# The fourth cross-attention head's probabilities turned by VectorE and put in place over DRAM, with its scores' maximum taken sooner

## The chip, the core and the metric

The kernel runs on one core of a Trainium2 chip. The metric is device time in microseconds (us) of one execution; lower is better. Five engines work side by side, each through its own list of instructions in order: TensorE (PE, with its weight loads as PEld), VectorE (DVE), ScalarE (ACT), GpSimd (POOL) and SyncE (SP, which here only issues DMAs). They wait for each other through semaphores.

## What is computed

The kernel is one decoder layer for 256 tokens of width 1024: a token mixer with causal attention, a cross-attention into 256 memory tokens, and a gated feed-forward network, each followed by a layer norm. All of it is float32. The change lies in the cross-attention alone, which has four heads of width 256:

```python
q = (h @ w_xq).reshape(B_, S_, XATTN_HEADS, XATTN_HEAD_DIM)
s = jnp.einsum('bshd,bmhd->bhsm', q, k, ...) * (XATTN_HEAD_DIM ** -0.5)
p = jax.nn.softmax(s, axis=-1)
o = jnp.einsum('bhsm,bmhd->bshd', p.astype(v.dtype), v).reshape(B_, S_, D)
return o @ w_xo
```

The scores and the probabilities `p` come out with the tokens on the partitions, and the product with `v` needs them with the memory tokens on the partitions. So each head's 256 x 256 probabilities have to be turned.

## The kernel before, in words

**Products.** A float32 product is made of three matmuls. Every operand is split into a high part (a cast on ACT, line 495 for activations and 148 for weights) and a low part (a subtraction on DVE, lines 496 and 150); `three` (lines 388 to 393) then issues high by high (L391), high by low (L392) and low by high (L393).

**The weight stream.** `Stream` keeps one list of weight tiles w0, w1, ... in order of use. SP loads raw tiles (L124, names like `w66r`) as the low half of an older tile has been made; ACT and DVE split them (`w59h`, `w59l`). Each step of a projection asks for its tile and, while the stream isn't held, splits one more, so the splits of the tiles to come stand in ACT's and DVE's lists between the work of the cross-attention. A high tile takes the room of one that TensorE has finished with.

**Order of the work.** Nothing reorders the instructions: the Python program is the order of every engine's list. `run(gen, n)` takes n steps of a projection's generator, and the calls between such steps are placed by hand.

**One head of the cross-attention** goes through these steps (h is its number, 0 to 3):

- `xscores(h)` (L1005 to 1017): twelve matmuls (L1012) into one PSUM bank `xs`; then `negmax` on DVE (L646, tile `mx`), `exps` on ACT (L635, two activations with their sums), and `scaled` on DVE (a reciprocal at L640 and two multiplications at L642), which leaves the probabilities in the tile `xpr`.
- `xprobs_out(h)` (heads 0 to 2): DVE turns the blocks of 32 x 32 into a tile `xs` (L527), and POOL issues the DMA of it to DRAM (`xd`, L530).
- `xprobs_in(h)` (heads 0 to 2): POOL waits for `xd` to have landed and issues four DMAs that bring the blocks back to SBUF in their places (`xr`, L538).
- `xprobs_split(h)` (heads 0 to 2): ACT casts `xr` into the high half of `xst` (L495), DVE makes the low half (L496).
- `xprobs_pe(h)` (head 3 alone) does in place of the three steps above: four transposes on TensorE into a PSUM bank `xpt` (L1035), which ACT and DVE split into `xst`.
- `xattend(h)`: twelve matmuls into a bank `xo` (L391 to 393), which ACT and DVE split into `oTh` and `oTl`.

The tiles `xs`, `xr` and `xst` share three buffers of one tag (`pair`); a new one takes a buffer whose last reader stands earlier in the program.

**The output projection** `xo` (L1071) takes the weight rows w51 to w54, for the outputs of heads 0 and 1, in its first eight steps, and w55 to w58 after the last head is there. The program around the change (L1070 to 1083) runs `xattend(0)`, `xprobs_split(1)`, `xscores(3)`, `xprobs_in(2)`, two steps, `xattend(1)`, four steps, `xprobs_split(2)`, `xprobs_pe(3)`, two steps, `xattend(2)`, `xattend(3)`, and then the rest of the projection with the second layer norm.

Of the kernel before, what the change touches and what calls it, by code (L numbers as in the profile page):

```python
# [8 lines left out]
F32 = mybir.dt.float32  # L9
F32R = mybir.dt.float32r  # L10
# [4 lines left out]
P = 128  # L15
D = 1024
S = 256
T = S // P
# [15 lines left out]
PR_BUFS = 7  # L34
# [6 lines left out]
def r32(t):  # L41
    return t.bitcast(F32)


class Stream:
# [122 lines left out]
    def next(self):  # L168

        i = len(self.tiles)  # L170
        return i + (2 if i < len(self.items) and self.items[i][0] == "sums" else 1)
# [40 lines left out]
def decoder_layer(  # L212
# [3 lines left out]
    nc = tc.nc  # L216
# [3 lines left out]
    sp = ctx.enter_context(tc.tile_pool(name="small", bufs=3))  # L220
# [10 lines left out]
    def bank(name):  # L231
        return pb.tile([P, 512], F32, tag="b", name=name)
# [137 lines left out]
    ident = cp.tile([P, P], F32, name="ident")  # L370
# [17 lines left out]
    def three(ps, w, y, start, stop, part=False):  # L388

        (wa, wb), (ya, yb) = w, y  # L390
        nc.tensor.matmul(ps, wa, ya, start=start, stop=False, skip_group_check=part)  # L391
        nc.tensor.matmul(ps, wa, yb, start=False, stop=False, skip_group_check=part)  # L392
        nc.tensor.matmul(ps, wb, ya, start=False, stop=stop, skip_group_check=part)  # L393

    def pair(hl, *ix):
        return hl[0][ix], hl[1][ix]
# [89 lines left out]
    def run(gen, n=None):  # L486

        while n is None or n > 0:
            if next(gen, gen) is gen:
                return False  # L490
            n = None if n is None else n - 1
        return True

    def split(h, l, ps):
        nc.scalar.copy(h, ps)  # L495
        nc.vector.tensor_sub(l, ps, r32(h))  # L496
# [25 lines left out]
    def turned(blocks, n, name, queue=nc.sync):  # L522

        st = sp.tile([P, 4, n, 32], F32, name=f"{name}s", tag="pair", bufs=3)
        for at, src in blocks:
            m = src.shape[1]
            nc.vector.transpose(st[:, :, at:at + m, :].rearrange("p j m b -> p m j b"),  # L527
                                src.rearrange("p m (j b) -> p m j b", b=32))
        via = hp.tile([P, 4, n * 32], F32, name=f"{name}d")
        queue.dma_start(via, st.rearrange("p j m b -> p j (m b)"))  # L530
        return via

    def landed(via, n, name, queue=nc.sync, raw=None):

        if raw is None:
            raw = sp.tile([P, 4, n, 32], F32, name=f"{name}r", tag="pair", bufs=3)
        for j in range(4):
            queue.dma_start(raw[32 * j:32 * (j + 1)].rearrange("p i m b -> p i (m b)"),  # L538
                              via[:, j, :].rearrange("(i a) r -> a i r", i=4))
        return raw  # L540
# [91 lines left out]
    def exps(dst, src, mx, sign=1.0):  # L632
        sm = sp.tile([P, 2], F32, name="sm", bufs=6)
        for j in range(2):
            nc.scalar.activation(dst[:, j, :], src[:, j, :], AF.Exp, bias=mx[:, j:j + 1], scale=sign,  # L635
                                 accum_out=sm[:, j:j + 1])
        return sm

    def scaled(dst, sm):
        nc.vector.reciprocal(sm, sm)  # L640
        for j in range(2):
            nc.vector.tensor_scalar(dst[:, j, :], dst[:, j, :], sm[:, j:j + 1], None, op0=OP.mult)  # L642

    def negmax(src):
        mx = sp.tile([P, 2], F32, name="mx", bufs=6)
        nc.vector.tensor_reduce(mx, src, op=OP.max, axis=AX.X, negate=True)  # L646
        return mx
# [254 lines left out]
    def project(chunks, get, held, pieces=PIECES):  # L902

        acc = {piece: accbank("acc") for piece in PIECES}
        if pieces != PIECES:
            (*_, (_, _, c), _), last = pieces, PIECES[-1]
            acc[pieces[-2]], acc[pieces[-1]] = acc[last][:, :c - last[1]], bank("acc")[:, :last[2] - c]
        head, rest = chunks[:-held], chunks[-held:]  # L910
        done = sum(ws.rows(numbers) for numbers in head)
        if head:
            yield from proj_rows(acc, head, get, PIECES, True, pieces != PIECES, True)
        ws.prepare(ws.used + AHEAD)
        ws.held = True
        for piece in pieces:
            yield from proj_rows(acc, rest, lambda k: get(done + k), [piece], not head or piece[1] % 512 != 0, True,
                                 piece == pieces[-1], bool(head) and pieces != PIECES)
            yield piece, acc[last] if pieces != PIECES and piece == pieces[-2] else acc[piece]
# [77 lines left out]
    xqT, xpr, xpt, turnsx = {}, {}, {}, {}  # L997
# [7 lines left out]
    def xscores(h):  # L1005
        ps = bank("xs").rearrange("p (t s) -> p t s", t=2)
        for low in range(2):
            for t in range(T):
                for kk in range(2):
                    w = xqT[h][low][:, kk, t * P:(t + 1) * P]  # L1010
                    for n in range(2 - low):
                        nc.tensor.matmul(ps[:, t, :], w, xkT[n][:, 2 * h + kk], start=not (low or t or kk or n),  # L1012
                                         stop=bool(low and kk), skip_group_check=True)
        pr = sp.tile([P, 2, T, P], F32, name="xpr", tag="pr", bufs=PR_BUFS)
        by_t = pr.rearrange("p s t b -> p t s b")
        scaled(by_t, exps(by_t, ps.rearrange("p t (s b) -> p t s b", s=2), negmax(ps)))
        xpr[h] = pr

    def xprobs_out(h):
        turnsx[h] = turned([(0, xpr[h].rearrange("p s t b -> p (s t) b"))], 4, "x", nc.gpsimd)  # L1020

    def xprobs_in(h):
        turnsx[h] = landed(turnsx[h], 4, "x", queue=nc.gpsimd)

    def xprobs_split(h):
        raw = turnsx[h].rearrange("p i m b -> p m i b")
        st = sp.tile([P, 2, 2, S], F32R, name="xst", tag="pair", bufs=3)
        xpt[h] = st[:, 0], st[:, 1]
        split(*[x.rearrange("p s (t i b) -> p (s t) i b", t=T, i=4) for x in xpt[h]], raw)

    def xprobs_pe(h):
        pp = bank("xpt").rearrange("p (s t) -> p s t", s=2)
        for s in range(2):
            for t in range(T):
                nc.tensor.transpose(pp[:, s, t * P:(t + 1) * P], xpr[h][:, s, t, :], ident)  # L1035
        st = sp.tile([P, 2, 2, S], F32R, name="xst", tag="pair", bufs=3)
        xpt[h] = st[:, 0], st[:, 1]
        split(*xpt[h], pp)

    def xattend(h):  # L1040
        po = bank("xo").rearrange("p (d t) -> p d t", d=2)
        for dd in range(2):
            for s in range(2):
                c = h * 256 + dd * P
                three(po[:, dd, :], pair(xv, ALL, s, slice(c, c + P)), pair(xpt[h], ALL, s), s == 0, s == 1)
        split(oT[0][:, 2 * h:2 * h + 2, :], oT[1][:, 2 * h:2 * h + 2, :], po)
# [2 lines left out]
    run(xq[0])  # L1049
    xv_split(1)  # L1050
    run(xq[1], 5)
    xscores(0)
    xprobs_out(0)
    run(xq[1])
    run(xq[2], 3)
    xprobs_in(0)
    run(xq[2], 2)
    xscores(1)
    xprobs_out(1)
    run(xq[2])  # L1060
    run(xq[3], 3)
# [1 line left out]
    run(xq[3], 1)  # L1063
    xprobs_split(0)
    run(xq[3], 1)
    xscores(2)
    xprobs_out(2)
    run(xq[3])

    h2 = ap.tile([P, T, D], F32, tag="a8", name="h2")  # L1070
    xo = project(c_xo, lambda k: (oT[0][:, k], oT[1][:, k]), 4)  # L1071
    xattend(0)
    xprobs_split(1)
    xscores(3)
    xprobs_in(2)
    run(xo, 2)
    xattend(1)
    run(xo, 4)
    xprobs_split(2)
    xprobs_pe(3)  # L1080
    run(xo, 2)
    xattend(2)
    xattend(3)

# [376 lines left out]
```

## Time and profile before

| what | value |
|---|---|
| median of 3 runs | 363.35 us (363.15 to 363.68) |
| the profiled execution | 364.67 us, of which its span is 362.9 us |
| TensorE busy in the span | 357.4 us (98%) |
| VectorE busy | 313.8 us (86%) |
| ScalarE busy | 204.2 us (56%) |
| GpSimd busy | 76.9 us (21%) |
| granted clock of TensorE, mean | 0.998 |

The span is the part of the execution that the profile covers; the 1.8 us around it are not seen. Times in the rows below are us from the start of the span. The part that the change touches lies between 150 and 172 us. A matmul's busy time runs until its modelled end, and the next one has begun before that, so TensorE's pace is read from the starts of its matmuls.

### The profile page before, as it was taken

What the parts mean: (1) busy time and instruction counts of PE and PEld (TensorE: products, weight loads), DVE (VectorE), ACT (ScalarE), POOL (GpSimd) and SP (SyncE); (2) the same over time, 40 slices, a digit from 0 to 9 for tenths busy, and PEclk for the clock granted to TensorE, in tenths of its full rate; (3) what the DMA queues carried; (4) which work ended last, traced back from release to release, by engine and by line L of the source; (5) the groups of instructions that cost most, each with busy time, mean ns of one, the idle gap of its engine ahead of it and who ended that gap; (6) DMA issues with size and microseconds to landing.
All of it is one profiled execution on the core that took longest, in us unless ns stands there. A gap on an engine that the chain in (4) does not pass through costs nothing. (4 is left out here: it accounts for less than half of the span.)

```text
span 362.9 us, 5453 instructions
## 1 busy us (share of the span) xinstructions
PE 357.4 (98%) x1836; PEld 304.2 (84%) x1836; DVE 313.8 (86%) x481; ACT 204.2 (56%) x324; POOL 76.9 (21%) x92
## 2 busy tenths in 40 slices
PE   9999999999999999999999999999999999999994
PEld 8888888887888899988888878888888888888883
DVE  5878999984999898765879959999999999879995
ACT  5767776374462565464128617538646654675921
POOL 1000009400010003320010024054044123303283
PEclk9999999999999999999999999999999999999999
DMA  7997379697965996935105896798798789777113
GB/s 243 417 418 287 116 268 330 171 349 187 417 256 185 362 381 226 338 124 178 58 0 204 318 307 217 230 343 278 235 331 266 262 303 298 275 237 246 57 60 116
DMA packets 35771, 89.75 MB, mean 247 GB/s; under 512 B 4256, under 2 KB 14112, under 8 KB 35616
## 3 DMA queue, kind: packets, MB, share of 16 engines
q1 hardware_dynamic: 34688, 87.57, 68.5%
q0 software_dynamic: 624, 1.57, 1.3%
q8 instruction: 14, 0.23, 0.2%
q10 hardware_dynamic: 432, 0.26, 0.2%
q14 instruction: 13, 0.11, 0.1%
HBM read 82.05 MB, written 7.34 MB: 246 GB/s over the span
## 5 line engine op out<-in xcount | busy, mean ns | idle before, releaser
L1128 POOL TENSOR_TENSOR sraw<-gr 128x128 f32<-128x128 f32 x10 | 10.6, 1058 | 104.3 <-DMA gr<-gd 71.2
L878 POOL TENSOR_TENSOR rs<-mv,mhalf 128x1 f32<-128x1 f32 x6 | 3.8, 637 | 66.2 <-DVE mv L876 66.2
L731 POOL TENSOR_TENSOR win<-upad 128x271 f32<-128x271 f32 x4 | 3.5, 880 | 52.7 <-DVE upad L765 52.7
L1129 POOL TENSOR_TENSOR sraw<-sraw,gr 128x128 f32<-128x128 f32 x10 | 12.1, 1205 | 0.8
L496 DVE TENSOR_TENSOR gTl<-gr,gTh 128x512 fp32r<-128x512 f32 x11 | 8.6, 779 | 2.7 <-ACT gTh L495 2.7
L495 ACT CAST h2Th<-tp 128x512 fp32r<-128x512 f32 x4 | 2.2, 587 | 14.5 <-PE tp L515 7.6
L495 ACT CAST S<-sraw 128x384 fp32r<-128x384 f32 (+1 forms) x10 | 5.3, 534 | 8.8 <-POOL sraw L1130 8.8
L495 ACT CAST gTh<-gr 128x512 fp32r<-128x512 f32 x11 | 6.8, 617 | 5.0 <-DMA gr<-gd 5.0
L530 POOL DMA_DIRECT2D xd<-xs x3 | 1.9, 628 | 33.2 <-DVE xs L527 33.2
L1108 ACT ACTIVATE sg<-pg 128x256 f32<-128x256 f32 x22 | 7.6, 378 | 1.7 <-PE pg L393 1.7
L1109 DVE TENSOR_TENSOR sg<-sg,pg 128x256 f32<-128x256 f32 x22 | 8.4, 414 | 0.1
L538 POOL DMA_DIRECT2D xr<-xd x12 | 6.6, 556 | 8.9 <-DMA xd<-xs 6.5
L635 ACT ACTIVATE xpr<-xs,mx 128x256 f32<-128x256 f32 x8 | 3.7, 469 | 8.3 <-DVE mx L646 8.3
L635 ACT ACTIVATE pr<-pr,mx 128x256 f32<-128x256 f32 (+1 forms) x12 | 5.5, 460 | 4.4 <-DVE mx L681 4.4
L527 DVE STREAM_TRANSPOSE gs<-sg 128x512 f32<-128x512 f32 x11 | 7.7, 702 | 0.1
L1133 POOL TENSOR_TENSOR S<-gr,sraw 128x128 f32<-128x128 f32 x8 | 7.6, 950 | 0.0
L1130 POOL TENSOR_TENSOR sraw<-gr 128x128 f32<-128x128 f32 x10 | 7.6, 760 | 0.0
L883 DVE SCALAR_TENSOR_TENSOR r<-r,mv,g 128x512 f32<-128x512 f32 (+1 forms) x10 | 7.0, 730 | 0.2
L164 POOL TENSOR_TENSOR w138l<-t,w138h 128x1024 fp32r<-128x1024 f32 x1 | 4.2, 4209 | 13.1 <-ACT w138h L163 13.1
L496 DVE TENSOR_TENSOR S<-sraw,S 128x384 fp32r<-128x384 f32 (+1 forms) x10 | 5.8, 576 | 1.3 <-ACT S L495 1.3
L776 ACT COPY pr<-pxk 128x256 f32<-128x256 f32 x8 | 2.6, 378 | 7.2 <-PE pxk L431 7.2
L869 DVE BATCH_NORM_STATS2 st<-r 128x6 f32<-128x512 f32 (+1 forms) x10 | 6.4, 637 | 0.3
(1399 smaller groups left out, 1421.8 us busy)
## 6 DMA issues: line engine op xcount, KB each, us to landing
gd<-gs SPq DMA_DIRECT2D x11, 256.0 KB, 5.8
gr<-gd SPq DMA_DIRECT2D x44, 64.0 KB, 2.0
pd<-ps SPq DMA_DIRECT2D x4, 384.0 KB, 4.3
pt<-pd SPq DMA_DIRECT2D x16, 96.0 KB, 7.2
g<-in_ln_g SPq DMA_DIRECT2D x3, 512.0 KB, 6.0
b<-in_ln_b SPq DMA_DIRECT2D x3, 512.0 KB, 7.7
wr<-in_w_qkv SPq DMA_DIRECT2D x5, 256.0 KB, 4.5
mr<-in_mem_t SPq DMA_DIRECT2D x1, 1024.0 KB, 11.5
```

What stands on the lines that cost most here:

```text
L495: nc.scalar.copy(h, ps)
L496: nc.vector.tensor_sub(l, ps, r32(h))
L527: nc.vector.transpose(st[:, :, at:at + m, :].rearrange("p j m b -> p m j b"), src.rearrange("p m (j b) -> p m j b", b=32))
L538: queue.dma_start(raw[32 * j:32 * (j + 1)].rearrange("p i m b -> p i (m b)"), via[:, j, :].rearrange("(i a) r -> a i r", i=4))
L635: nc.scalar.activation(dst[:, j, :], src[:, j, :], AF.Exp, bias=mx[:, j:j + 1], scale=sign, accum_out=sm[:, j:j + 1])
L883: nc.vector.scalar_tensor_tensor(r, r, self.mv[:, 0:1], gb["g", self.i][:, s], op0=OP.subtract, op1=OP.mult)
L1108: nc.scalar.activation(sg, ps[:, :CW].rearrange("p (f b) -> p f b", f=2), AF.Silu, bias=0.0, scale=1.0)
L1109: nc.vector.tensor_mul(sg, sg, ps[:, CW:].rearrange("p (f b) -> p f b", f=2))
L1128: nc.gpsimd.tensor_add(s1, a21, a22)
L1129: nc.gpsimd.tensor_sub(s2, s1, a11)
L1130: nc.gpsimd.tensor_sub(s3, a11, a21)
L1133: nc.gpsimd.tensor_sub(s4_raw, a12, s2)
```

## The change

Head 3 gets the same steps as the other three: `xprobs_out(3)`, `xprobs_in(3)` and `xprobs_split(3)` stand for `xprobs_pe(3)`, which is gone. `xscores` is cut in two: the call issues the matmuls and the maximum, and what it returns issues the exponentials and the scaling. For heads 0 to 2 both are called at once. For head 3 the split of head 1's probabilities stands between them, so that on DVE the maximum comes before that split. The four steps after `xattend(1)` are taken as two and two, with `xprobs_in(3)` between, and the split of head 3's probabilities comes after the last two steps, not before them.

```diff
--- before.py
+++ after.py
@@ -1011,10 +1011,15 @@
                     for n in range(2 - low):
                         nc.tensor.matmul(ps[:, t, :], w, xkT[n][:, 2 * h + kk], start=not (low or t or kk or n),
                                          stop=bool(low and kk), skip_group_check=True)
-        pr = sp.tile([P, 2, T, P], F32, name="xpr", tag="pr", bufs=PR_BUFS)
-        by_t = pr.rearrange("p s t b -> p t s b")
-        scaled(by_t, exps(by_t, ps.rearrange("p t (s b) -> p t s b", s=2), negmax(ps)))
-        xpr[h] = pr
+        mx = negmax(ps)
+
+        def softmax_rest():
+            pr = sp.tile([P, 2, T, P], F32, name="xpr", tag="pr", bufs=PR_BUFS)
+            by_t = pr.rearrange("p s t b -> p t s b")
+            scaled(by_t, exps(by_t, ps.rearrange("p t (s b) -> p t s b", s=2), mx))
+            xpr[h] = pr
+
+        return softmax_rest
 
     def xprobs_out(h):
         turnsx[h] = turned([(0, xpr[h].rearrange("p s t b -> p (s t) b"))], 4, "x", nc.gpsimd)
@@ -1027,15 +1032,6 @@
         st = sp.tile([P, 2, 2, S], F32R, name="xst", tag="pair", bufs=3)
         xpt[h] = st[:, 0], st[:, 1]
         split(*[x.rearrange("p s (t i b) -> p (s t) i b", t=T, i=4) for x in xpt[h]], raw)
-
-    def xprobs_pe(h):
-        pp = bank("xpt").rearrange("p (s t) -> p s t", s=2)
-        for s in range(2):
-            for t in range(T):
-                nc.tensor.transpose(pp[:, s, t * P:(t + 1) * P], xpr[h][:, s, t, :], ident)
-        st = sp.tile([P, 2, 2, S], F32R, name="xst", tag="pair", bufs=3)
-        xpt[h] = st[:, 0], st[:, 1]
-        split(*xpt[h], pp)
 
     def xattend(h):
         po = bank("xo").rearrange("p (d t) -> p d t", d=2)
@@ -1049,13 +1045,13 @@
     run(xq[0])
     xv_split(1)
     run(xq[1], 5)
-    xscores(0)
+    xscores(0)()
     xprobs_out(0)
     run(xq[1])
     run(xq[2], 3)
     xprobs_in(0)
     run(xq[2], 2)
-    xscores(1)
+    xscores(1)()
     xprobs_out(1)
     run(xq[2])
     run(xq[3], 3)
@@ -1063,22 +1059,26 @@
     run(xq[3], 1)
     xprobs_split(0)
     run(xq[3], 1)
-    xscores(2)
+    xscores(2)()
     xprobs_out(2)
     run(xq[3])
 
     h2 = ap.tile([P, T, D], F32, tag="a8", name="h2")
     xo = project(c_xo, lambda k: (oT[0][:, k], oT[1][:, k]), 4)
     xattend(0)
+    rest = xscores(3)
     xprobs_split(1)
-    xscores(3)
+    rest()
     xprobs_in(2)
+    xprobs_out(3)
     run(xo, 2)
     xattend(1)
-    run(xo, 4)
+    run(xo, 2)
+    xprobs_in(3)
+    run(xo, 2)
     xprobs_split(2)
-    xprobs_pe(3)
     run(xo, 2)
+    xprobs_split(3)
     xattend(2)
     xattend(3)
 
```

## Rows read from the trace of the kernel before

**Rows 1.** TensorE's waits in the whole span: us in total, times, longest.

```profile
PE busy L550 <- PEq L1425: 0.8, 1, 0.8
PE left L1402 <- ACT mean L1375: 0.5, 1, 0.5
```

**Rows 2.** Timeline of PE: start, us, engine, line, operation, tiles, count.

```profile
163.76 0.39 PE L393 MATMUL acc<-w53h,oTl 128*128 128x512 f32 x1
163.98 0.60 PE L1035 MATMUL xpt<-ident,xpr 128*128 128x128 f32 x4
164.34 0.48 PE L391 MATMUL acc<-w54h,oTh 128*128 128x512 f32 x1
164.65 0.40 PE L392 MATMUL acc<-w54l,oTh 128*128 128x512 f32 x1
164.89 0.40 PE L393 MATMUL acc<-w54h,oTl 128*128 128x512 f32 x1
```

**Rows 3.** Timeline, 150 to 160 us; brackets: idle before, and what ended it.

```profile
150.57 0.71 DVE L527 STREAM_TRANSPOSE xs<-xpr 128x512 f32<-128x512 f32 x1
...
151.58 0.56 POOL L530 DMA_DIRECT2D xd<-xs  x1 [2.29 <-DVE xs L527]
...
153.73 0.64 PE L1012 MATMUL xs<-xkTh,xq 128*128 128x256 f32 x4
...
155.63 0.62 ACT L495 CAST xst<-xr 128x512 fp32r<-128x512 f32 x1 [2.07 <-DMA xr<-xd]
...
156.23 2.17 POOL L538 DMA_DIRECT2D xr<-xd  x4 [4.09 <-DMA xd<-xs]
...
156.28 0.69 DVE L496 TENSOR_TENSOR xst<-xr,xst 128x512 fp32r<-128x512 f32 x1 [2.00 <-ACT xst L495]
...
156.89 0.69 DVE L646 TENSOR_REDUCE mx<-xs 128x2 f32<-128x512 f32 x1
...
157.62 0.47 ACT L635 ACTIVATE xpr<-xs,mx 128x256 f32<-128x256 f32 x1 [1.36 <-DVE mx L646]
...
158.87 0.62 DVE L642 TENSOR_SCALAR xpr<-xpr,sm 128x256 f32<-128x256 f32 x2
```

**Rows 4.** Landings of xd (all three); then xr of heads 0, 1, 2, issues (ns).

```profile
DMA to landing us min/median/max: 2.4/2.6/4.1
...
L538 POOL DMA_DIRECT2D xr<-xd x4: 548/558/608, 141.3 to 143.0; - x4
...
DMA to landing us min/median/max: 2.4/3.0/3.3
...
L538 POOL DMA_DIRECT2D xr<-xd x4: 548/548/553, 147.1 to 148.7; - x4
...
DMA to landing us min/median/max: 6.3/6.5/6.7
...
DMA to landing us min/median/max: 2.1/2.1/2.2
```

**Rows 5.** Busy us by stretch: PE, PEld, DVE, ACT, POOL; PEclk, DMA share, GB/s.

```profile
140.00:145.00 5.00, 5.00 (x44) 5.00 (x44) 3.84 (x8) 2.62 (x7) 2.81 (x5) 1.00 0.82 270
145.00:150.00 5.00, 5.00 (x44) 5.00 (x43) 3.42 (x7) 2.82 (x7) 2.17 (x4) 1.00 0.91 333
...
164.00:166.00 2.00, 2.00 (x12) 1.74 (x11) 1.01 (x2) 1.38 (x2) 0.00 (x0) 1.00 0.85 295
```

**Rows 6.** Timeline, 160 to 169 us; SPq is SP's DMA queue.

```profile
160.86 0.33 SPq L124 DMA_DIRECT2D w66r<-in_w_gu  x1
...
161.40 1.06 ACT L148 CAST w61h<-w61r 128x1024 fp32r<-128x1024 f32 x1 [0.40 <-PE acc L393]
...
165.10 1.05 ACT L148 CAST w62h<-w62r 128x1024 fp32r<-128x1024 f32 x1
...
166.19 1.23 DVE L150 TENSOR_TENSOR w62l<-w62r,w62h 128x1024 fp32r<-128x1024 f32 x1 [0.26 <-ACT w62h L148]
...
168.75 0.28 PE L392 MATMUL xo<-xst,xv 128*128 128x256 f32 x1
```

## The prediction

> **What bounds the kernel now.** I first read the list of TensorE's waits. It has three lines over the whole span, and the two longest are 0.8 and 0.5 us [rows 1]: TensorE is almost never without work, and none of the three lines belongs to the cross-attention or the feed-forward network. So TensorE's instruction list sets the time. A matmul taken off that list shortens the kernel by its own pitch; work added to another engine costs nothing until TensorE waits for it. The next views were TensorE's timeline around the transposes [rows 2], for the prize, and the timelines of ACT, DVE, POOL and SP from 150 to 169 us with the landings of head 0 to 2's DMAs, to see whether the longer way for head 3 still ends before TensorE asks for it.
>
> **What is removed: four transposes on TensorE.** From the last matmul of w53 to the second of w54 there are 0.89 us (163.76 to 164.65); without the transposes these would be two pitches of 0.24 us (164.65 to 164.89) [rows 2]. So 0.89 - 0.48 = 0.41 us come off TensorE's list. The bounds are 0.36 us (start of the transposes to start of the next matmul) and their busy time of 0.60 us. Nothing hides this: before and after, TensorE goes from one matmul to the next, so all that follows moves forward by 0.41 us if no new wait appears. The split of head 3's probabilities into high and low parts stays, one cast and one subtraction of the same shape, only with a source in SBUF in place of PSUM; I cost that at nothing.
>
> **What is moved: the maximum.** Head 3's scores end at 153.73 + 0.64 = 154.37. DVE then stood idle for 2.00 us until head 1's low half at 156.28, and the maximum came behind that, at 156.89 [rows 3]. Put ahead, it runs from 154.4 to 155.1, inside the idle time, and delays nothing behind it. ACT's next item is still the cast at 155.63, which waits for head 1's blocks from DRAM; the exponentials start behind it, at 155.63 + 0.62 = 156.25, where they started at 157.62: 1.37 us sooner. Were that gain lost, every time below would move later by up to 1.37.
>
> **What is added: DVE's turn, one DMA out, four in.** The scaling ended at 158.87 + 0.62 = 159.49 [rows 3]; 1.37 sooner is 158.12. The turn takes 0.71 us on DVE (158.83). Behind it on DVE stand the split of w59 and head 1's low output, which profit by 1.37 us and give back 0.71. POOL issues the DMA 0.30 us after the turn (head 2: turn over at 151.28, issue at 151.58): 159.13. POOL is free by then; head 2's four issues end at 156.23 + 2.17 = 158.40. That DMA lands 2.6 us later (heads 0 to 2: 2.4 to 4.1) [rows 4]: 161.73, and POOL starts the four loads 0.55 us behind a landing (head 2: 151.58 + 4.1 = 155.68, start 156.23), at 162.28. The last of the four is issued 1.65 us after the first (141.3 to 143.0 and 147.1 to 148.7), at 163.93.
>
> How long that last load takes is the one large unknown. Head 2's took 2.1 to 2.2 us, head 0's 2.4 to 3.3, head 1's 6.3 to 6.7 [rows 4]. The DMA engines' share beside them was 0.82 for head 0 and 0.91 for head 1, and it is 0.85 between 164 and 166 us [rows 5]. That is nearest to head 0, so I take its median of 3.0 and keep 2.1 and 6.7 as ends. It gives 166.9. ACT starts a cast about 0.2 us behind a landing (head 1: 148.7 + 6.7 = 155.4, cast at 155.63): 167.1. SP's queue is not touched, but its loads are paced by DVE: w66, issued at 160.86 once DVE was done with w59 [rows 6], goes out up to 0.9 us sooner and meets the DMA to DRAM; that is in the range of 2.4 to 4.1.
>
> **What stands ahead on ACT and DVE, and what TensorE waits for.** The new split comes behind the split of w62. ACT stood idle for 0.40 us until TensorE released a tile for w61's cast at 161.40 [rows 6]; w62's waits likewise for w53, whose last matmul ends at 163.76 + 0.39 = 164.15. So it starts near 164.2 in place of 165.10, takes 1.05 us and leaves ACT free at 165.3; DVE has done its half (1.23 us, [rows 6]) by 166.5. Neither holds back a cast at 167.1. From cast to low half ready there are 0.65 + 0.69 = 1.34 us (155.63 to 156.28, then the subtraction) [rows 3]: 168.44. TensorE's second matmul of head 3's product with v reads that low half; it stood at 168.75 [rows 6], now 168.75 - 0.41 = 168.34. So TensorE waits 0.10 us, and the sum is -0.41 + 0.10 = -0.31 us. Behind the late cast on ACT and DVE stand head 2's outputs, needed only behind head 3's product, so they add no wait of their own.
>
> The profiled execution took 364.67 us, 362.9 of it span, 1.3 above the median of 363.35; the sum concerns the span and I take it off the median: 363.35 - 0.31 = 363.04.
>
> **A rule against it.** While head 0's four loads were issued, DVE was busy for 3.84 of 5 us [rows 5], and an issue took 548 to 608 ns, against 548 to 553 for head 1 [rows 4]: 60 ns at most of hindrance. The Trainium skill, SBUF — State Buffer, section on the two separate sides, warns that GpSimd can be locked out by some VectorE instructions, so that a DMA issued from its queue waits for its descriptors, and names about 620 ns alone against about 3100 beside a copy. By that figure, as an estimate, one such DMA would cost 2.5 us more and the kernel would come out slower. The trace of heads 0 to 2 does not bear it out.
>
> **The rivals.**
> - *All hidden.* The last load lands as head 2's did, 2.1 to 2.8 us after its issue; the cast starts by 166.9 and nothing waits: -0.41, up to -0.6 with the larger bound: 362.75 to 362.95. For it: the weight loads are spread wider once w66 and w67 go out sooner. I count it with the forecast, since the two differ by less than the runs do; likewise a wait of up to 0.41.
> - *The way over DRAM is late.* Weight loads hold up the four loads, or the DMA out. The point from which it decides is a landing 3.3 us after the last issue: then TensorE's wait of 0.4 eats the prize, and each further tenth is lost in full. With head 2's 4.1 out and head 0's 3.3 in, the cast comes at 168.9 and the wait is 1.9: 363.35 - 0.41 + 1.9 = 364.8. With head 1's 6.7 in, the cast comes at 170.8 and the wait is 3.8: 366.7. For it: a DMA share of 0.85 there. Against it: head 0, with 0.82, stayed at 3.3, and only the 0.91 beside head 1 went with 6.7 [rows 4, 5].
> - *POOL's issues are held by DVE.* Each of the five issues could wait for a DVE instruction of up to 1.23 us, that of w62's size; three of them waiting in full put the cast at 170.8, a wait of 3.8: 366.7. Against it: the 60 ns above. It is the mechanism that the page of the Trainium skill named above describes.
> - *The maximum isn't really sooner.* Something on DVE or ACT keeps the exponentials at 157.62; the cast then comes 1.37 later, at 168.5, a wait of 1.5: 364.4. Against it: 2.00 us of idle DVE at the right place.
> - *More than the transposes.* Earlier splits on ACT and DVE take further small waits off TensorE. Its list of waits has nothing in the stages from here to the last layer norm, so I see at most 0.1 us more; a gain beyond 0.73 would have no source that I can name.
>
> **How the numbers follow.** Forecast with its hidden end and with waits up to 0.41: 0.72, its own range 362.8 to 363.35. DRAM way late: 0.16, of which 0.06 ends within 0.73 us of before. Held issues: 0.02. Maximum not sooner: 0.04. More than that: 0.06. A measurement of this kernel can tell about 0.2%, 0.73 us, from no change. Faster by over that: 0.06. Slower: 0.10 + 0.02 + 0.04 - 0.02 (a maximum only partly sooner stays within) = 0.14. The same: 0.80. The range goes from 362.7 (the larger bound of the prize) to 364.2, into the late cases until about 0.15 is left out.
>
> **What would show it.** After: no transposes at L1035; w54's matmuls directly behind w53's at 0.23 to 0.24 us; the maximum near 154.5 and the exponentials near 156.25; a DMA to DRAM near 159.1; four loads from 162.3 to 164.4; the cast of head 3 between 166.4 and 167.5; the gap of TensorE ahead of head 3's product at most some tenths. A gap of over 0.4 us there, or loads that land more than 3.3 us after issue, makes the forecast of a small gain wrong; a gain of over 0.7 us would show a wait of TensorE that I haven't seen.

## The result: slower by 0.66%, where a gain of 0.1% was forecast

| | median | runs | spread |
|---|---|---|---|
| before | 363.46 us | 7 | 363.15 to 364.47 |
| after | 365.55 us | 7 | 364.73 to 367.28 |

The ratio of after to before is 1.0066, with a 95% interval of 1.0051 to 1.0081. The forecast was 363.04 us in a range from 362.7 to 364.2, with a chance of 0.14 for slower by over 0.2%. The median lies 1.35 us above the upper end of the range. The spread is a result too: the seven runs of the kernel before lie within 1.3 us, those of the changed one within 2.6.

The profiled execution of after took 364.95 us with a span of 362.8, against 364.67 and 362.9 before. Two things stand behind these numbers. The time outside the span, which no trace shows, grew: it is 1.7 to 1.9 us in all 79 executions of before whose span is on record, and 2.1 to 2.2 us in all 18 of after, 0.37 us more in the mean. So of the 2.1 us between the medians some 0.4 lie outside the span. And against that execution of after, that of before had lost 0.5 us ahead of the cross-attention and 0.3 behind it, so the two traces can't be compared by their ends. The cross-attention alone can be compared, from the first matmul of head 0's scores to the first of w59 (the feed-forward network): 181.87 - 131.45 = 50.42 us before, 182.11 - 130.92 = 51.19 us after.

**The profile after.** The page's busy times, and its line of the DMA queue that POOL issues to (packets, MB, share of the 16 engines):

```profile
PE 356.4 (98%) x1832; PEld 304.1 (84%) x1832; DVE 315.1 (87%) x482; ACT 205.2 (57%) x324; POOL 78.9 (22%) x97
q0 software_dynamic: 832, 2.10, 1.8%
```

TensorE's list of waits over the whole span of after (in total, times, longest), which answers to [rows 1]:

```profile
PE busy L550 <- PEq L1425: 0.8, 1, 0.8
PE xo L391 <- ACT xst L495: 0.6, 1, 0.6
PE left L1402 <- ACT mean L1375: 0.5, 1, 0.5
PE xo L392 <- DVE xst L496: 0.3, 1, 0.3
```

Two lines are new, and both say `xo` and `xst`: TensorE waits for the high half (ACT) and then for the low half (DVE) of a head's turned probabilities. The timeline of PE shows where. First the place where the transposes were [rows 2], then the seam between head 2's and head 3's product (start, us, engine, line, operation):

```profile
163.02 0.39 PE L393 MATMUL acc<-w53h,oTl 128*128 128x512 f32 x1
163.24 0.39 PE L391 MATMUL acc<-w54h,oTh 128*128 128x512 f32 x1
163.47 0.39 PE L392 MATMUL acc<-w54l,oTh 128*128 128x512 f32 x1
...
167.28 0.28 PE L393 MATMUL xo<-xst,xv 128*128 128x256 f32 x1
168.18 0.38 PE L391 MATMUL xo<-xst,xv 128*128 128x256 f32 x1 [0.62 <-ACT xst L495]
168.90 0.38 PE L392 MATMUL xo<-xst,xv 128*128 128x256 f32 x1 [0.34 <-DVE xst L496]
```

The prize is there: w54 follows w53 at 0.22 to 0.23 us. But these products start every 0.12 us, and the two marked starts come 0.90 and 0.72 behind the one ahead. TensorE waits 0.78 + 0.61 = 1.39 us. (The brackets say less, since they count from the modelled end of the last matmul.)

The chain that ends there, from the timelines of DVE, ACT and POOL, answers to [rows 3]:

```profile
153.80 0.69 DVE L646 TENSOR_REDUCE mx<-xs 128x2 f32<-128x512 f32 x1
...
155.09 0.47 ACT L635 ACTIVATE xpr<-xs,mx 128x256 f32<-128x256 f32 x1
...
156.99 0.71 DVE L527 STREAM_TRANSPOSE xs<-xpr 128x512 f32<-128x512 f32 x1
...
158.00 0.56 POOL L530 DMA_DIRECT2D xd<-xs  x1 [0.34 <-DVE xs L527]
161.10 1.09 POOL L538 DMA_DIRECT2D xr<-xd  x2 [2.54 <-PE acc L393]
162.35 1.09 POOL L538 DMA_DIRECT2D xr<-xd  x2
...
163.44 1.05 ACT L148 CAST w62h<-w62r 128x1024 fp32r<-128x1024 f32 x1 [1.15 <-PE acc L393]
167.50 0.62 ACT L495 CAST xst<-xr 128x512 fp32r<-128x512 f32 x1 [3.01 <-DMA xr<-xd]
```

The landings of head 3's DMA out, and the issues (ns) and landings of its four loads, which answer to [rows 4]:

```profile
DMA to landing us min/median/max: 2.4/2.4/2.4
...
L538 POOL DMA_DIRECT2D xr<-xd x4: 548/550/553, 161.1 to 162.9; - x4
...
DMA to landing us min/median/max: 4.2/4.4/4.5
```

The reader is to see that everything up to the four loads was in time, and that ACT, done with w62 at 164.5, then stood idle for 3.01 us until the last of them landed. They took 4.2 to 4.5 us, the last 4.5; the sum had 3.0.

### The profile page after: what moved, and what is told of

The parts are those of the page before. It is cut to its first block, busy times and chain, and to the rows that moved or that the text cites. A ratio compares the mean times of both kernels' runs of the same rounds, so it can differ in the third digit from the quotient of the medians.

```text
span 362.8 us, 5464 instructions
## 1 busy us (share of the span) xinstructions
PE 356.4 (98%) x1832; PEld 304.1 (84%) x1832; DVE 315.1 (87%) x482; ACT 205.2 (57%) x324; POOL 78.9 (22%) x97
## 5 line engine op out<-in xcount | busy, mean ns | idle before, releaser
L1128 POOL TENSOR_TENSOR sraw<-gr 128x128 f32<-128x128 f32 x10 | 8.8, 875 | 103.3 <-DMA gr<-gd 76.4
L538 POOL DMA_DIRECT2D xr<-xd x16 | 8.8, 557 | 11.6 <-ACT xst L495 4.2
L1130 POOL TENSOR_TENSOR sraw<-gr 128x128 f32<-128x128 f32 x10 | 11.0, 1097 | 0.0
L1129 POOL TENSOR_TENSOR sraw<-sraw,gr 128x128 f32<-128x128 f32 x10 | 10.7, 1066 | 0.8
L1012 PE MATMUL xs<-xkTh,xq 128*128 128x256 f32 x32 | 6.4, 283 | 0.0
```

Of the source, the lines that this page charges most:

```text
L1128: nc.gpsimd.tensor_add(s1, a21, a22)
L1129: nc.gpsimd.tensor_sub(s2, s1, a11)
L1130: nc.gpsimd.tensor_sub(s3, a11, a21)
```

## The experiments

Theory A: TensorE waits for head 3's halves, since its four loads land late, and they land late because of the weight loads beside them. Rival B: the way over DRAM is too long in itself, whatever else is on the DMA engines. Rival C: the time is lost elsewhere, and the wait is only a part of it. All edits are to the changed kernel, where nothing else is said.

**The changed kernel again, eight traces in all.** Nothing is edited.

> The changed kernel once more, to see how its loss is spread. Theory A (TensorE waits for head 3's low and high halves, because the four loads from DRAM land late): the wait of TensorE ahead of head 3's product, 1.4 us in the first trace, is found again and is larger in a longer execution; 364.7 to 367.3 us. Rival C (the time is lost elsewhere, the wait is only a part of it): the wait stays near 1.4 us in a longer execution and other gaps of TensorE make up the rest.

It took 366.5 us in the median of 5 runs (363.99 to 367.99), ratio 1.0068 (1.0040 to 1.0097). But its traced execution was the shortest of the five, with the same wait as the first. So more single executions were traced, for a long one.

> The changed kernel, one more look, for an execution longer than the two traced so far (waits of 1.38 us, spans 361.8 and 362.8). Theory A: in an execution of 365 us and more of span, the loads of head 3 land 5 us or more after their issue, the wait of TensorE is 3 us or more, and its granted clock falls behind that wait as in the run with the late maximum. Rival C: the wait is again 1.4 us and the longer time lies elsewhere.

> As the look before it: another execution of the changed kernel, same expectations.

These two were short ones as well (364.14 and 364.77). Four more followed:

> The changed kernel; if this execution is over 366 us, theory A expects loads that land 6 us or so after their issue, a wait of TensorE of 3 us or more and a granted clock of about a half for some 2 us behind it; rival C expects the wait of 0.9 to 1.4 us again and the rest elsewhere.

> The changed kernel once more; for an execution over 366 us the same expectations as for the look before this one.

> The changed kernel once more; for an execution over 366 us the same expectations as for the two looks before this one.

> The changed kernel once more; for an execution over 366 us the same expectations as for the three looks before this one.

The eight executions, in order of the wait. "Wait" is what the first two starts of head 3's product come late, as worked out above; "stage" runs from head 0's scores to w59; "clock" is the lowest granted clock in any 2 us from 160 to 178 us.

| time | loads' landing, min to max | wait | stage | clock |
|---|---|---|---|---|
| 364.14 | 3.2 to 4.0 | 0.89 | 50.71 | 1.00 |
| 364.77 | 3.2 to 4.2 | 1.09 | 50.91 | 1.00 |
| 364.95 | 4.2 to 4.5 | 1.39 | 51.19 | 1.00 |
| 363.99 | 3.9 to 4.5 | 1.39 | 51.21 | 1.00 |
| 365.59 | 3.7 to 5.0 | 1.93 | 51.73 | 1.00 |
| 367.45 | 4.2 to 4.8 | 2.12 | 53.69 | 0.50 |
| 368.25 | 4.3 to 5.4 | 2.75 | 54.24 | 0.50 |
| 368.73 | 2.8 to 3.3 | 3.06 | 54.36 | 0.50 |

Up to a wait of 1.93 the stage is 49.72 us (the same stage without any wait, from the runs below) plus the wait plus 0.1. In the last three it is 1.5 to 1.7 us more than that. (The four longest of the eight were all taken on one chip, so the chip may have a part in the spread; but the five runs from 363.99 to 367.99 come from one chip as well.) The execution of 368.25 us shows where the rest comes from. Its timeline of PE, and its busy times by stretch (PE, PEld, DVE, ACT, POOL; then granted clock, DMA share, GB/s):

```profile
167.46 0.28 PE L393 MATMUL xo<-xst,xv 128*128 128x256 f32 x1
169.72 0.38 PE L391 MATMUL xo<-xst,xv 128*128 128x256 f32 x1 [1.99 <-ACT xst L495]
170.45 0.38 PE L392 MATMUL xo<-xst,xv 128*128 128x256 f32 x1 [0.34 <-DVE xst L496]
...
172.24 0.63 PE L391 MATMUL acc<-w55h,oTh 128*128 128x512 f32 x1
172.67 0.63 PE L392 MATMUL acc<-w55l,oTh 128*128 128x512 f32 x1
```

```profile
168.00:170.00 2.00, 0.28 (x1) 0.19 (x1) 0.29 (x1) 0.94 (x2) 0.00 (x0) 1.00 0.63 238
170.00:172.00 2.00, 1.66 (x11) 1.55 (x11) 1.00 (x2) 0.16 (x1) 0.00 (x0) 0.84 0.04 12
172.00:174.00 2.00, 2.00 (x8) 1.61 (x7) 0.69 (x1) 1.52 (x2) 0.00 (x0) 0.50 0.00 0
```

TensorE was busy for 0.28 us of the two from 168 to 170. Behind that the granted clock fell to 0.50, its lower level of 1.2 GHz, and w55's matmuls came every 0.43 us, not every 0.23, until the clock was back between 174 and 176. So in these executions a late landing is paid twice, once as the wait and once as slow matmuls behind it. That is the case in the longest executions alone: of the 12 in the two groups of runs, the mean granted clock was 0.994 or 0.995 in the four from 367.12 us up, and 0.997 to 0.999 in the other eight, those at the two medians among them. Rival C falls for the larger part of the spread, since the long executions are those with the long wait (363.99 and 364.95, with the same wait, differ by 1 us elsewhere). It holds for the 0.37 us outside the span, which every execution of after has. The last one of the table was late for another reason. Its loads landed in 3.3 us at most, but they could not be issued before 165.00. Head 2's DMA out had taken 5.4 us (4.1 before), and POOL, which issues in order, came to head 3's DMA out at 159.60. That one took 4.7 us; the load of w66 was issued 0.15 us behind it, where 0.6 to 0.8 us lay between them in the other seven traces, with 2.4 to 2.5 us to its landing:

```profile
159.60 0.56 POOL L530 DMA_DIRECT2D xd<-xs  x1
165.00 1.09 POOL L538 DMA_DIRECT2D xr<-xd  x2 [4.84 <-issue]
```

**The weight loads wait for head 3's loads.**

```diff
     xattend(1)
-    run(xo, 2)
     xprobs_in(3)
-    run(xo, 2)
+    seen = hp.tile([P, 2], F32, name="seen")
+    nc.sync.dma_start(seen, turnsx[3][:, 0, 0, 0:2])
+    run(xo, 4)
```

> POOL's loads stay, but SP waits for them to have landed before it loads w67, w68 and w69 (a small DMA that reads from all four parts stands ahead on SP's queue); only w66 can run beside them. Theory A with traffic as the cause: landings 2.1 to 2.6 us after the issue as for head 2, no wait of TensorE ahead of head 3's product, 363.0. Rival B: landings still over 4 us, 365 to 366. If the postponed weight loads themselves come late, TensorE waits for w67 or w68 after 182 us instead.

It took 363.36 us, ratio 0.9998 (0.9986 to 1.0011). Landings of the four loads, ACT's cast behind them, and SP's queue:

```profile
DMA to landing us min/median/max: 2.1/2.2/2.3
```

```profile
166.12 0.62 ACT L495 CAST xst<-xr 128x512 fp32r<-128x512 f32 x1 [1.13 <-DMA xr<-xd]
...
166.18 0.33 SPq L1078 DMA_DIRECT2D seen<-xr  x1
166.60 0.38 SPq L124 DMA_DIRECT2D w67r<-in_w_gu  x1
```

The same four loads, issued by the same engine as late as 162.0 to 163.8, land in 2.1 to 2.3 us once w67 and w68 aren't beside them, and head 3's wait is gone. Theory A with traffic as the cause stands, and rival B falls. The weight loads, held back by up to 6 us, are missed by nobody: TensorE has no new wait behind them. The stage took 50.21 us in this trace, 0.49 over the one without a wait, as it held 0.3 us of another wait, for head 1's low half, and 0.1 of a slower start behind it.

**Only w68 and w69 wait.** The small DMA stands behind w67 on SP's queue.

```diff
     xprobs_in(3)
+    seen = hp.tile([P, 2], F32, name="seen")
+    nc.sync.dma_start(seen, turnsx[3][:, 0, 0, 0:2])
     run(xo, 2)
```

> As the run in which the weight loads wait, but only w68 and w69 wait for head 3's four loads; w66 and w67 run as in the changed kernel. Tells which load does the harm. If w68, issued just behind them, is what slows them down: landings 2 to 2.6 us after the issue and no wait, 363.3. If w67, still in flight when they are issued, is what they share the DMA engines with: landings of 3 to 4 us, a wait of some tenths to 1 us, 363.7 to 364.5.

It took 364.02 us, ratio 1.0008 (0.9989 to 1.0026), with a wait of 0.31 us in its trace. Issues and landings of the four loads, and the cast behind them:

```profile
L538 POOL DMA_DIRECT2D xr<-xd x4: 548/548/556, 161.5 to 163.3; - x4
...
DMA to landing us min/median/max: 3.0/3.9/4.3
```

```profile
166.42 0.62 ACT L495 CAST xst<-xr 128x512 fp32r<-128x512 f32 x1 [1.93 <-DMA xr<-xd]
```

The first of the four took 4.3 us and the last 3.0, and the cast needs all four. With w67 and w68 both held back, the last took 2.2; with neither held back, 4.0 to 5.4 in the seven executions above in which it was the loads that were slow. So w67, in flight when the loads are issued, holds up the first of them most and the last by 0.8 us; by the last load, by the wait and by the time the greater part of the harm is w68's, which is issued just behind them. That is one trace of a time that spreads, so the two shares are not measured closely.

**Head 3's loads from SP's queue, in the same place.**

```diff
-    xprobs_in(3)
+    xprobs_in(3, nc.sync)
```

(Here and in the next run `xprobs_in` takes the queue as an argument; POOL's is the default.)

> Only the queue of head 3's four loads changes, from POOL to SP, where they stand behind the load of w67 and ahead of w68. Theory A with traffic as the cause (weight loads issued beside them slow them down): they land 2 to 3 us after their issue, near 165, two us sooner than 167.3; the wait of TensorE goes, and the kernel is 0.4 us under before, 363.0. Rival B (the chain is too long in itself, whatever else is on the DMA engines): landings stay 4 us and more after the issue and the kernel stays at 365 to 366.

A miss for the form of theory A that I had written down: 364.16 us, ratio 1.0016 (1.0002 to 1.0030), wait 1.02 us, and the landings were no sooner than from POOL:

```profile
DMA to landing us min/median/max: 4.4/4.8/5.0
```

SP issues faster (the four loads within 1.3 us of each other, from 161.54, where POOL takes 1.8), but w67's 512 KB (161.04) stand directly ahead of them here too. By the landings it is not the issuing engine that counts. The Trainium skill, DMA: Bandwidth & Descriptors, section on issuing engines not being separate DMA queues, says the same: transfers started by any engine run on the same 16 DMA engines and interleave. This trace agrees, with 4.8 us from SP's queue against 4.4 from POOL's.

The times say more than that one trace, though. On the same chip the changed kernel took 366.5 us (ratio 1.0068, 1.0040 to 1.0097), so the queue alone took off most of the loss. Some 0.3 us of that lie outside the span (1.87 against 2.16 in the mean), and none of the 12 executions has a mean granted clock under 0.996. Why the long executions stay away the one trace doesn't show.

**Head 3's loads first on SP's queue, ahead of w66.**

```diff
     xprobs_out(3)
+    xprobs_in(3, nc.sync)
...
-    run(xo, 2)
-    xprobs_in(3)
-    run(xo, 2)
+    run(xo, 4)
```

> Head 3's four loads go to SP's queue right behind its DMA out, ahead of the loads of w66, w67 and w68, which SP then issues about 2 us later. Theory A with traffic as the cause: nothing is in flight beside the four loads, they land about 2 us after their issue, near 163.5, the split of w62 and not the landing is what ACT has ahead of head 3's cast, and TensorE doesn't wait: 0.41 us under before, ratio 0.9989. Rival B (the chain is too long in itself): a wait of TensorE ahead of head 3's product stays, and the kernel is slower than before.

It took 363.33 us against 363.84 for before on the same chip, ratio 0.9986 (0.9977 to 0.9996), in 12 runs from 362.72 to 364.08. On that chip this version is a little faster than before, by 0.04 to 0.23%. Its landings, and SP's and ACT's rows:

```profile
DMA to landing us min/median/max: 1.8/1.9/2.0
```

```profile
160.99 1.75 SPq L538 DMA_DIRECT2D xr<-xd  x4
162.84 0.38 SPq L124 DMA_DIRECT2D w66r<-in_w_gu  x1
...
164.44 0.62 ACT L495 CAST xst<-xr 128x512 fp32r<-128x512 f32 x1
```

ACT's cast now follows w62's with no wait. That is 1.7 us before it is needed: in the first trace of after the second matmul of head 3's product followed the cast by 1.40 us (168.90 behind 167.50), and here it starts at 167.55, so a cast at 166.15 would have done. The stage takes 49.72 us. SP stands waiting for the DMA out, and w66 goes out at 162.84 in place of 158.84, which costs nothing.

**The prize by itself.** Head 3 takes head 2's probabilities; its turn, its DMA out and its loads are left out.

```diff
-    xprobs_out(3)
...
-    xprobs_in(3)
...
+    turnsx[3] = turnsx[2]
     xprobs_split(3)
```

> Head 3 takes head 2's probabilities, so its turn, its DMA out and its four loads are left out; its split stays, and the transposes of TensorE are gone. It measures the prize by itself: 0.41 us under before, ratio 0.9989, with no wait of TensorE in the cross-attention. If more than the transposes' pitch comes off, 0.7 us or more under before.

It took 363.21 us, ratio 0.9981 (0.9971 to 0.9991), that is 0.7 us off, and its stage of 49.72 us is the same as with the loads first on SP's queue. So that version gets the whole prize inside the span. By time it gets less, 0.5 us, since it spends 2.17 us outside its span in the mean, and this run 1.80.

**The sooner maximum alone, on the kernel before.**

```diff
+    rest = xscores(3)
     xprobs_split(1)
-    xscores(3)
+    rest()
```

(`xscores` is cut in two here as in the changed kernel.)

> The kernel before with the sooner maximum alone; head 3 is still turned by TensorE. Theory A: head 3's chain was not waited for, so nothing changes, 363.4 within 0.3. Rival C (the sooner maximum or its place on DVE and ACT costs something): 364 or more.

As expected, it can't be told from before: 363.6 us, ratio 0.9995 (0.9986 to 1.0005). Its stage was 50.21 us, 0.2 under that of before in one trace each, so at most that.

**The changed kernel with the maximum where it was.**

```diff
-    rest = xscores(3)
     xprobs_split(1)
-    rest()
+    xscores(3)()
```

> The changed kernel with head 3's maximum where it was, behind head 1's split on DVE. Theory A: the whole way of head 3, exponentials, turn, DMA out and loads, is 1.4 us later, and so is its cast; TensorE's wait grows from 1.4 to 2.8 us, less what the loads then find less traffic; some 1 us slower than the changed kernel. Rival B': another thing than the chain sets the cast, and the wait stays at 1.4 us.

It took 369.71 us, ratio 1.0167 (1.0144 to 1.0191). By the two ratios that is 3.7 us more than the changed kernel, not 1; they were taken on different chips. The loads are issued 1.5 us later, but they also take longer, and the clock falls. Landings, TensorE's wait, and one stretch:

```profile
DMA to landing us min/median/max: 4.4/6.3/6.8
```

```profile
PE xo L391 <- ACT xst L495: 3.6, 1, 3.6
```

```profile
172.00:174.00 2.00, 2.00 (x9) 2.00 (x10) 0.53 (x1) 0.00 (x0) 0.00 (x0) 0.50 0.04 8
```

From the first issue, at 162.6 in place of 161.1, w67 (162.03) and w68 (163.17) are now both just ahead of them or among them.

**The loads first on SP's queue, with the late maximum.** The two edits together.

> The version with head 3's loads first on SP's queue, and the maximum back behind head 1's split. Theory A: with loads that land 2 us after their issue there is slack, 164.4 for the cast against a last moment near 166.9, so 1.4 us later still costs no wait: ratio 0.9986 to 0.9995, no wait of TensorE in the cross-attention. If the sooner maximum is needed even so, a wait of some tenths shows ahead of head 3's product and the time is that of before or more.

It took 363.47 us, ratio 0.9998 (0.9989 to 1.0006), which can't be told from before; 0.9986 to 0.9995 was expected. By its trace there is no wait in the cross-attention, the cast of head 3 starts at 164.30 and the stage takes 49.72 us, as with the sooner maximum. The slack is shown; whether the sooner maximum is worth anything then, the times don't tell.

**The time outside the span.** It is 2.1 to 2.2 us in after, in the version with the late maximum and in both versions with the loads first on SP's queue. It is 1.7 to 1.9 us in before, in the version with the sooner maximum alone, in the one that measures the prize and in the two with the small DMA on SP's queue; with the loads on SP's queue in the same place it is 1.8 to 2.1. So it goes with the version and not with the chip. What it consists of no trace shows, and the cause stays open.

## Why the prediction was wrong

- *TensorE bounds the kernel, and the transposes come off it.* Right; the size was a little low. The sum had 0.41 us. The stage without transposes and without a wait is 49.72 us against 50.21 with the maximum sooner and the transposes there, 0.49, and the run that measures the prize alone gave 0.7 with an interval from 0.3 to 1.1 us.
- *The maximum moves into an idle hole of DVE, and costs nothing.* Right: it ran right behind the scores, and the exponentials followed head 1's cast directly, 155.09 behind 154.57.
- *The way out.* Right, and even sooner. Against the start of head 0's scores, which came 0.53 us sooner in the trace of after, the four loads began 0.65 us before the forecast (161.10 + 0.53 = 161.63, forecast 162.28).
- *The last load takes 3.0 us.* This is the term that failed. It was taken from head 0 "as nearest", because the DMA engines' share was 0.82 beside head 0 and 0.85 here [rows 5]. The eight traces show the last of the four loads at 4.0 to 5.4 us in seven, and a DMA out of 4.7 us in the eighth. The share was the wrong row to go by. In stretches of 2 us of the trace before, head 0's loads (140 to 146) stand beside 0.93, 0.87 and 0.56, and the place for head 3's (162 to 168) has 0.79, 0.85 and 0.55, so by that row they should have been no slower. One stretch of each (DMA share next to last):

```profile
142.00:144.00 2.00, 2.00 (x19) 2.00 (x18) 1.56 (x5) 1.27 (x3) 1.57 (x3) 1.00 0.87 291
...
162.00:164.00 2.00, 2.00 (x11) 1.56 (x10) 2.00 (x3) 0.97 (x2) 0.00 (x0) 1.00 0.79 277
```

  Head 0 was also a model of one trace. Its slowest load took 3.3 us there, the least of all 17 traces, in which it goes up to 4.8. A nearer row is which weight loads are in flight and how long they take themselves, and it stood in the trace of before. The list of its DMA issues, first beside head 0's loads (138 to 152 us), then where head 3's were to go (159 to 167 us), with size and us to landing:

```profile
w61r<-in_w_gu SPq DMA_DIRECT2D x1, 512.0 KB, 3.3
w62r<-in_w_gu SPq DMA_DIRECT2D x1, 512.0 KB, 3.6
...
w64r<-in_w_gu SPq DMA_DIRECT2D x1, 512.0 KB, 6.0
...
w67r<-in_w_gu SPq DMA_DIRECT2D x1, 512.0 KB, 4.2
w68r<-in_w_gu SPq DMA_DIRECT2D x1, 512.0 KB, 4.5
```

  In the trace of before, head 0's loads took 2.4 to 3.3 beside 3.3 and 3.6, and head 1's 6.3 to 6.7 beside w64's 6.0 (and beside a load of the layer norm's `b`). Head 3's took 4.2 to 4.5 in the first trace of after, where before had 4.2 and 4.5. This is read after the fact and was not tested, and it is no rule: head 2's loads took 2.1 us beside the last 0.6 us of w65's 4.4, which speaks for what is still to come of a weight load, not its whole time. With 4.4 for 3.0 the wait would have been 1.5 us and the sum 1.1 us slower than before. The five shorter executions have waits of 0.9 to 1.9.
- *A wait costs its own length.* It did up to 1.93 us. Behind the three longest waits of the table, and in the run with the late maximum, the granted clock fell to half, for another 1.5 to 1.7 us. The prediction didn't price that. It makes the executions over 367 us; the medians have the clock of the short ones.
- *The sum concerns the span and is taken off the median.* This put the change of the time outside the span at nothing, and gave no reason. It grew by 0.37 us.
- Together: the traced execution nearest to the median of 365.55 us took 365.59. Its stage is 1.3 us longer than that of before, and with the 0.37 that is 1.7 of the 2.1 us. The rest is less than the remaining span differs from one execution to the next (310.6 to 312.5 us in the 17 traces).
- *w66 goes out up to 0.9 us sooner and meets the DMA out.* It went out sooner still: 158.84 for 160.86, 1.5 us against the start of head 0's scores. w67 came sooner with it (160.80 for 162.59) and so stood just ahead of the four loads. In one of eight traces the DMA out took 4.7 us against 2.4, with w66 issued directly behind it; that w66 was the cause was not tested.
- *POOL's issues held by DVE.* They weren't: 548 to 553 ns for each of the four loads in the first trace.
- The rival that came true is "the way over DRAM is late". Its mechanism and its place were right. Its 364.8 us was the nearer number, though it came from a slow DMA out, and in seven of eight traces it was the loads. Its chance of 0.16 was too small, since it, too, was weighed by the DMA share.

## What to carry to other kernels

Before moving work onto a DMA way with little slack, look up in the trace which transfers will be in flight beside it, and in more than one trace how long such a way takes; the DMA engines' busy share didn't tell here. A transfer that someone waits for belongs ahead of the prefetches, which can wait: put on the prefetches' own queue in front of them, it took 1.9 us rather than 4.4, and the change turned from a loss of 0.7% into a gain of 0.14% (0.04 to 0.23%, on one chip). Where TensorE is the bound, a wait of over 2 us is to be priced with the slower matmuls behind it, as it was here. And a forecast for the whole time needs a look at what lies outside the span.

## What the runs showed of the hardware that was not expected

- A DMA's time to land beside others spreads from one execution to the next, with the same program: 4.0 to 5.4 us for the slowest of the same four loads in seven traces, against 1.8 to 2.3 us where w67 and w68 were held back behind them.
- A chain whose loads were issued 1.5 us later came out 3.7 us later by the ratios: the loads took longer (4.4 to 6.8 us) and TensorE's clock fell behind the longer wait.
- Behind waits of 2.1 to 4.4 us TensorE was granted half its clock for a time (0.84, 0.50 and 0.80 in three stretches of 2 us in the execution of 368.25 us), with matmuls of 512 columns every 0.43 us; behind those of 0.9 to 1.9 us it kept 1.00.
- The time outside the span differed between versions of one kernel, 1.7 to 1.9 us or 2.1 to 2.2 us, on every chip alike. The cause is open.
